# First loads in pieces on two queues, low halves of the first weights on VectorE, and another last stage, in a two-layer encoder kernel

## The chip, the cores and the metric

The kernel runs on one core of a Trainium2 chip. The metric is the time of one execution on the device in microseconds (us); a profile of one execution shows what each engine did. PE is TensorE, DVE VectorE, ACT ScalarE, POOL GpSimd, and SP the engine whose queue issues most transfers (DMAs).

## What is computed

Two layers over 1024 tokens of width 1024, in float32: windowed attention in layer 0, neighbourhood attention in layer 1, each with four heads over 256 memory tokens beside it, and a gated feed-forward part. The parts that the change touches:

```python
mem_n = rmsnorm(mem, norm_mem)
for i in range(DEPTH):                      # 2
    h = rmsnorm(x, norm_mix[i])
    mkv = mem_n @ w_mem_kv[i]               # keys and values of the memory
    proj = h @ (w_in_a if i % 2 == 0 else w_in_b)[i // 2]
    ...                                     # attention
    x = x + concat(y_tok, y_mem) @ w_out[i]
    h = rmsnorm(x, norm_ffn[i])
    gu = h @ w_gate_up[i]
    x = x + (silu(gu[..., :D_FF]) * gu[..., D_FF:]) @ w_down[i]
return rmsnorm(x, norm_final)
```

## The kernel before

**Layout.** Activations lie transposed: tile `x[k][f]` holds features 128k to 128k+127 of token half f (512 tokens). A product is made from operands split into a high half (float32r) and the rest: `hi` copies on ACT, `lo` subtracts (on DVE, or on POOL where `eng=nc.gpsimd` is given, then in four pieces), and each 128x128 block costs three matmuls (`three`). The tools' tile scheduler fixes each engine's instruction order when the program is built, and each engine works through its order without overtaking. SP issues the loads in its own order, and one that waits for a free buffer holds those behind it.

**Opening.** The pool `mp` holds the memory tokens `memt`. Eight units of memory keys and values follow (`i` from 0 to 7 in the loop): load a weight tile (`wm`, 512 KB, `load_w`), 24 matmuls of 256 columns against `mhl` (`dense`), scaling by `mscale` (`mt`), and for the value units a transpose (`mvT`, `mv`). Between them x is loaded and squared. The class `Norm` makes a root mean square: `add` squares a tile on ACT (`sq`) and merges it on DVE into two accumulators; `scale` merges these, sums over the partitions with matmuls against `inv_d` (`st`), adds epsilon (`nv`), takes the power on POOL (`nr`), builds a diagonal (`diag`) and broadcasts it by matmuls (`bc`). `split` then gives `h` and its halves `hT`. `first_dense` runs three units of the input projection on token half 0 (weights `wf`) while token half 1 is normalized; the same three units on half 1 follow, then the attention (scores `S`, probabilities `p`, transposes `pT`).

**End.** The down projection is done with seven products (`i` from 0 to 6, a Strassen scheme) of six groups of rows (`g` from 0 to 5). `left_side` loads and splits the weights (`wd_raw`, `wd`), `right_side` the operands (`b_raw`, `hB`), both two groups ahead. Weight tiles `wd` stand in a ring of three, raw tiles (`raw_tile`) in a ring of five here and of three in the opening. In the last group `product` runs over the four row blocks `m`, and `read` adds each block to x and hands it to `Norm`. `finish` scales a token half by `norm_final` and writes it in four pairs of tiles (512 KB each), all issued by SP, from a ring of two tiles `o`.

Of the kernel before, what the change touches and what calls it, by code (L numbers as in the profile page):

```python
# [41 lines left out]
def trunk_kernel(ctx: ExitStack, tc: tile.TileContext, a: dict, out: bass.AP):  # L42
# [110 lines left out]
    def first_dense(layer, norm):  # L153

        pre = []
        src = a["w_in_a"] if layer == 0 else a["w_in_b"]
        todo = (norm.add(x[k][1]) for k in range(len(norm.xs), NK))
        parts = norm.split(layer, hT[1])
        for n, u in enumerate(FIRST[layer]):
            w = load_w(src[u], eng=nc.gpsimd, name="wf")  # L160
            wide[:] = True, 2 + n
            ps = mm_tile()
            for i, _ in enumerate(steps(ps, w, hT[0])):
                if next(todo, 0) is not None and len(norm.xs) == NK and (n or i > 3):
                    next(parts, None)
            pre.append((w, ps))
        run(parts)
        return pre
# [15 lines left out]
    class Norm:  # L184


        def __init__(self, n=HS):
            self.n, self.acc, self.xs = n, [], {}

        def add(self, xk, k=None):  # L190

            n = self.n
            self.xs[len(self.xs) if k is None else k] = xk
            sq = temp("sq", n)
            nc.scalar.activation(sq, xk, AF.Square)
            self.acc.append(sq)
            if len(self.xs) > 2:
                self.merge()

        def merge(self):  # L200
# [4 lines left out]
        def scale(self):  # L205

            n, nb = self.n, self.n // P
            self.merge()
            st = ps_t.tile([P, HS], F32, tag="T", name="st")
            for b in range(nb):  # L210
                nc.tensor.matmul(
                    st[:, b : b + 1], self.acc[0][:, b * P : (b + 1) * P], inv_d, start=True, stop=True
                )
            v = sp.tile([P, 4], F32, tag="nv", name="nv", bufs=2)
# [40 lines left out]
    with tc.tile_pool(name="mp", bufs=1, reuse_waits="tile") as mp:  # L255
        phase[:] = mp, 5, 3
        memt = mp.tile([P, NK, NM], F32, name="memt")
        nc.sync.dma_start(gains, a["gains"])
        nc.sync.dma_start(memt[:, : NK // 2], a["mem"][:, : NK // 2])
        ws = [load_w(a["w_mem"][0, 0], name="wm", parts=2)]  # L260
        nc.sync.dma_start(memt[:, NK // 2 :], a["mem"][:, NK // 2 :])
        nc.sync.dma_start(ident, a["ident"])

# [3 lines left out]
        for k in range(NK):  # L267
# [4 lines left out]
            )  # L272
            mh.append(t)
        ws.append(load_w(a["w_mem"][0, 1], name="wm"))
        mem_norm = Norm(NM)
        for k in range(NK):
# [7 lines left out]
        for i in range(8):  # L284
# [6 lines left out]
            if i + 2 < 8:  # L291
                ws.append(load_w(a["w_mem"][(i + 2) // 4, (i + 2) % 4], name="wm", eng=nc.gpsimd))
            if i == 0:
                nc.sync.dma_start(sink, a["sink"].to_broadcast([P, NH]))
                nc.vector.tensor_scalar(nsink, sink, -1.0, None, op0=ALU.mult)
            if i in (0, 3):
                f = i // 3
                for k in range(NK):
                    x[k][f] = mp.tile([P, HS], F32, tag=f"x{k}{f}", name=f"x0_{k}{f}")
                    nc.sync.dma_start(x[k][f], a["x"][k][:, f * HS : (f + 1) * HS])  # L300
            ps = dense(ws[i], mh, NM)
# [5 lines left out]
            else:  # L307
# [5 lines left out]
                for b in range(2):  # L313
                    hi(vm[:, b, m : m + 2, 0], src[:, b])
                    lo(vm[:, b, m : m + 2, 1], src[:, b], vm[:, b, m : m + 2, 0])
            if i in (1, 2, 3, 4):
                for k in (2 * i - 2, 2 * i - 1):
                    norms[0].add(x[k][0])
            if i == 4:
                parts = norms[0].split(0, hT[0])  # L320
            if i >= 4:
                run_some(parts, 2)
                for k in (2 * i - 8, 2 * i - 7):
                    norms[1].add(x[k][1])
# [6 lines left out]
    for layer in range(2):  # L331
# [427 lines left out]
        with tc.tile_pool(name=f"fp{layer}", bufs=1, reuse_waits="tile") as fp:  # L759
# [381 lines left out]
            def finish(norm, at):  # L1141

                bc = norm.scale()
                for k in range(NK):
                    if k % 2 == 0:
                        o = fp.tile([P, 2, HS], F32, tag="S", bufs=2, name="o")
                    nc.vector.scalar_tensor_tensor(
                        o[:, k % 2], norm.xs[k], gains[:, 5, k : k + 1], bc, op0=ALU.mult, op1=ALU.mult
                    )
                    if k % 2 == 1:  # L1150
                        nc.sync.dma_start(out[k - 1 : k + 1].rearrange("k p t -> p k t")[:, :, at : at + HS], o)
                    yield
# [12 lines left out]
            for at_, (i, g) in enumerate(dorder):  # L1165
# [22 lines left out]
                if i == 6:  # L1188
# [98 lines left out]
```

## Time and profile before

| | |
|---|---|
| three runs, us | 2201.31, 2204.14 (median), 2206.15 |
| profiled execution: time, span, us | 2205.49, 2202.5 |
| PE busy in the span | 2129.8 us (97%) |
| DVE, ACT, POOL busy | 1440.2, 1056.5, 673.9 us (65, 48, 31%) |

The span is what the profile shows from the first to the last instruction of the one execution; its time is 3.0 us longer. Busy times are averages over stages: what an edit is worth is read from the stage in which it lies. In the sections below an idle time and what ended it stand in square brackets at the end of a row.

### The profile page before, as it was taken

Reading aid. Unit: us, or ns where it says so; the run is one execution under the profiler, and the core shown is the slowest. Engines: PE = TensorE matmul, PEld = TensorE weight load, DVE = VectorE, ACT = ScalarE, POOL = GpSimd, SP = SyncE. Lnnn points to the kernel's source line nnn. Section 1 sums busy time; section 2 is a strip of 40 time slices with the busy share of each in tenths; the row PEclk is TensorE's granted clock in tenths of the full one; section 3 lists DMA queues with packets and bytes.
Section 4 is the critical chain, followed back from the end, with each engine's and each line's share of the span. In section 5 each row is a group of like instructions: output and inputs, shape, how many; then the busy total and the mean of one; then the engine's idle time right before and its main releaser. Section 6 shows DMA issues by size and latency. Waiting matters only on the chain.

```text
span 2202.5 us, 28160 instructions
## 1 busy us (share of the span) xinstructions
PE 2129.8 (97%) x9930; PEld 1749.9 (79%) x9930; DVE 1440.2 (65%) x2241; ACT 1056.5 (48%) x2016; POOL 673.9 (31%) x647
## 2 busy tenths in 40 slices
PE   6899999999999999999999999999999999999996
PEld 6688888788888887787788888887888888877875
DVE  5677787776555456767866666667865555567575
ACT  5477785443333333445466566653433333334442
POOL 4334330323332321363233233202233233213540
PEclk8999999999999999999999999999999999999998
DMA  6312117423223236766332222274232232366562
GB/s 221 119 39 82 49 58 268 133 82 122 97 93 110 100 115 225 248 208 215 111 91 72 76 65 86 64 263 139 82 101 110 96 115 96 120 225 229 178 234 81
DMA packets 117020, 287.21 MB, mean 130 GB/s; under 512 B 12304, under 2 KB 18704, under 8 KB 116880
## 3 DMA queue, kind: packets, MB, share of 16 engines
q1 hardware_dynamic: 110544, 273.89, 36.9%
q10 hardware_dynamic: 6336, 11.54, 1.4%
q8 instruction: 78, 1.28, 0.2%
q14 instruction: 62, 0.51, 0.1%
HBM read 210.40 MB, written 68.94 MB: 127 GB/s over the span
## 4 chain that ended last, share of the span: by engine, by line
PE 73%; issue 10%; DVE 6%; ACT 4%; DMA 4%; POOL 3%; SPq 0%; POOLq 0%; DVEq 0%; ACTq 0%
PE X L844 21%; PE Y L844 16%; PE mm L139 13%; PE X L1136 6%; PE po L139 4%; PE S L524 3%; PE Y L1136 3%; PE O L587 3%; PE pT L567 2%; DMA b_raw<-b_d 1%; DVE hB L109 1%; ACT p L539 1%; POOL x L1096 1%; DVE wd L109 1%; DMA wd_kept<-in_w_dn 1%
## 5 line engine op out<-in xcount | busy, mean ns | idle before, releaser
L844 PE MATMUL X<-hT,wgu 128*128 128x512 f32 x1056 | 259.0, 395 | 0.0
L844 PE MATMUL Y<-hB,wgu 128*128 128x512 f32 x1056 | 256.3, 392 | 0.0
L1136 PE MATMUL X<-hB,wd 128*128 128x512 f32 x1056 | 248.3, 395 | 7.0 <-DVE c L852 3.4
L844 PE MATMUL X<-hB,wgu 128*128 128x512 f32 x1056 | 247.8, 390 | 0.0
L1136 PEld LDWEIGHTS X<-hB,wd 128*128 128x128 f32 x1056 | 200.2, 190 | 52.9 <-DVE c L852 4.3
L844 PEld LDWEIGHTS X<-hT,wgu 128*128 128x128 f32 x1056 | 198.2, 188 | 47.2
L552 POOL TENSOR_SCALAR p<-p,stat 128x384 f32<-128x384 f32 (+1 forms) x256 | 140.9, 570 | 309.8 <-DVE stat L549 206.6
L844 PEld LDWEIGHTS Y<-hB,wgu 128*128 128x128 f32 x1056 | 198.5, 188 | 43.9 <-issue 1.5
L844 PEld LDWEIGHTS X<-hB,wgu 128*128 128x128 f32 x1056 | 198.3, 188 | 41.8
L106 ACT CAST wgu<-wS 128x1024 fp32r<-128x1024 f32 x88 | 92.5, 1051 | 259.7 <-POOL wS L803 157.1
L109 DVE TENSOR_TENSOR wgu<-wgu_raw,wgu 128x1024 fp32r<-128x1024 f32 (+1 forms) x88 | 85.7, 974 | 190.3 <-ACT wgu L106 190.3
L139 PE MATMUL mm<-hT,wqk 128*128 128x512 f32 x672 | 199.8, 405 | 0.1
L1136 PE MATMUL Y<-hB,wd 128*128 128x512 f32 x792 | 185.2, 395 | 8.9 <-DVE hB L109 4.5
L803 POOL TENSOR_TENSOR wS<-wgu_raw 128x512 f32<-128x512 f32 x44 | 73.6, 1672 | 379.0 <-DVE wgu L109 379.0
L139 PE MATMUL po<-yT,wo 128*128 128x512 f32 x768 | 184.7, 394 | 0.0
L1136 PEld LDWEIGHTS Y<-hB,wd 128*128 128x128 f32 x792 | 150.6, 191 | 42.6 <-DVE hB L109 5.3
L109 DVE TENSOR_TENSOR hB<-b_raw,hB 128x512 fp32r<-128x512 f32 x154 | 131.9, 892 | 53.1 <-ACT hB L106 52.9
L139 PEld LDWEIGHTS po<-yT,wo 128*128 128x128 f32 x768 | 142.4, 188 | 29.5 <-issue 1.0
L109 DVE TENSOR_TENSOR wgu<-wS,wgu 128x1024 fp32r<-128x1024 f32 x88 | 109.7, 1247 | 62.6 <-ACT wgu L106 62.6
L539 ACT ACTIVATE p<-p,stat 128x256 f32<-128x256 f32 (+1 forms) x192 | 112.4, 586 | 51.1 <-DVE stat L535 48.5
L810 POOL TENSOR_TENSOR wS<-wgu_raw 128x512 f32<-128x512 f32 x44 | 58.3, 1326 | 251.2 <-DMA wgu_raw<-in_w_gu 197.5
L106 ACT CAST hB<-b_raw 128x512 fp32r<-128x512 f32 x154 | 88.8, 619 | 95.4 <-DMA b_raw<-b_d 95.3
(158 smaller groups left out, 4026.8 us busy)
## 6 DMA issues: line engine op xcount, KB each, us to landing
wgu_raw<-in_w_gu SPq DMA_DIRECT2D x92, 512.0 KB
b_raw<-b_d SPq DMA_DIRECT2D x70, 512.0 KB
wd_raw<-in_w_dn SPq DMA_DIRECT2D x50, 512.0 KB
b_d<-c SPq DMA_DIRECT2D x88, 256.0 KB
b_d<-t SPq DMA_DIRECT2D x66, 256.0 KB
wo_raw<-in_w_out SPq DMA_DIRECT2D x32, 512.0 KB
wd_kept<-in_w_dn SPq DMA_DIRECT2D x10, 1024.0 KB
x<-in_x SPq DMA_DIRECT2D x32, 256.0 KB
```

The costliest lines, as they stand in the source:

```text
L106: nc.scalar.copy(dst, src)
L109: (eng or nc.vector).tensor_tensor(dst, src, h.bitcast(F32), op=ALU.subtract)
L139: nc.tensor.matmul(ps[:, :n], l, r, start=start and i == 0 and j == 0, stop=stop and i == len(order) - 1 and j == 2,)
L524: nc.tensor.matmul(s_[:, :n], Q[self.h][:, qb * P : (qb + 1) * P], k, start=j == 0, stop=j == 1)
L539: nc.scalar.activation(p[:, :n], p[:, :n], AF.Exp, bias=m1, scale=-1.0, accum_out=s1)
L552: nc.gpsimd.tensor_scalar(p[:, :n], p[:, :n], ri[:, i : i + 1], 1.0, op0=ALU.mult, op1=ALU.mult)
L567: nc.tensor.transpose(tr[:, j * P : (j + 1) * P], p[:, j * P : (j + 1) * P], ident)
L587: nc.tensor.matmul(o[:, c0 : c0 + w * P], self.value(j), t[:, s0 : s0 + w].rearrange("p j q -> p (j q)"), start=j == js[0] and t is self.p ...
L803: sub = lambda o, p_, q_: nc.gpsimd.tensor_tensor(o, p_, q_, op=ALU.subtract)
L810: nc.gpsimd.tensor_tensor(s[:, HS:], u1, u2, op=ALU.add)
L844: nc.tensor.matmul(ps, l, r, start=n in (0, 1, 3, 6) and k == 0 and i == 0, stop=k == 3 and i == 2, skip_group_check=True,)
L1136: nc.tensor.matmul(bank, l, r, start=i in (0, 1, 3, 6) and p == 0 and n == 0, stop=p == HF - 1 and n == 2, skip_group_check=True,)
```

## The change

In the opening the memory tokens come in three pieces (two, two and four of the eight feature blocks) instead of two halves, the first weight tile in two halves issued by ACT, and the table of ACT's functions is loaded by a small square of a constant tile ahead of any data. The low halves of the memory weights and of layer 0's first three projection weights are made on DVE instead of POOL. The loads of x are spread over the units 0 to 6, token half 0 is squared at the units 1 and 2 (four tiles each), and its `split` starts after unit 2. The pool has 8 temporaries instead of 5 and 5 raw tiles instead of 3.

At the end, groups 4 and 5 of the last product are done block by block: all nine matmuls of one row block, then the next. In layer 1's last token half the eighth square isn't merged: both accumulators and that square go to PE, twelve matmuls against `inv_d` where there were four. The tiles `o` come from the ring of raw tiles; in the last half two of the eight products are made on POOL (from tiles already scaled by the gain on ACT, and from a copy `bs` of the broadcast), the last two tiles go out singly on SP and ACT, and the first pair goes out on ACT.

```diff
-            w = load_w(src[u], eng=nc.gpsimd, name="wf")
+            w = load_w(src[u], eng=None if layer == 0 else nc.gpsimd, name="wf")
...
     class Norm:
-        def __init__(self, n=HS):
-            self.n, self.acc, self.xs = n, [], {}
+        def __init__(self, n=HS, summed=NK):
+            self.n, self.acc, self.xs, self.st = n, [], {}, None
+            self.summed = summed
 
         def add(self, xk, k=None):
...
             nc.scalar.activation(sq, xk, AF.Square)
+            if len(self.xs) > self.summed:
+                while self.acc:
+                    self.mean(self.acc.pop(0))
+                self.mean(sq)
+                return
             self.acc.append(sq)
             if len(self.xs) > 2:
                 self.merge()
+
+        def mean(self, sq):
+
+            start = self.st is None
+            if start:
+                self.st = ps_t.tile([P, HS], F32, tag="T", name="st")
+            for b in range(self.n // P):
+                nc.tensor.matmul(
+                    self.st[:, b : b + 1], sq[:, b * P : (b + 1) * P], inv_d,
+                    start=start and b == 0, stop=True, skip_group_check=True,
+                )
...
         def scale(self):
...
+            if len(self.acc) > 1:
+                self.merge()
+            for sq in self.acc:
+                self.mean(sq)
+            st = self.st
...
-        phase[:] = mp, 5, 3
+        phase[:] = mp, 8, 5
         memt = mp.tile([P, NK, NM], F32, name="memt")
+        warm = mp.tile([P, P], F32, name="warm")
+        nc.scalar.activation(warm, ones, AF.Square)
+        wm0 = raw_tile("wm0")
+        nc.sync.dma_start(memt[:, :2], a["mem"][:, :2])
+        nc.scalar.dma_start(wm0[:, :HS], a["w_mem"][0, 0][:, :HS])
         nc.sync.dma_start(gains, a["gains"])
-        nc.sync.dma_start(memt[:, : NK // 2], a["mem"][:, : NK // 2])
-        ws = [load_w(a["w_mem"][0, 0], name="wm", parts=2)]
-        nc.sync.dma_start(memt[:, NK // 2 :], a["mem"][:, NK // 2 :])
-        nc.sync.dma_start(ident, a["ident"])
+        nc.sync.dma_start(memt[:, 2:4], a["mem"][:, 2:4])
+        nc.scalar.dma_start(wm0[:, HS:], a["w_mem"][0, 0][:, HS:])
+        nc.sync.dma_start(memt[:, 4:], a["mem"][:, 4:])
+        w0 = wp.tile([P, 2, D], F32R, tag="whl", name="wm", bufs=3)
...
-                ws.append(load_w(a["w_mem"][(i + 2) // 4, (i + 2) % 4], name="wm", eng=nc.gpsimd))
+                ws.append(load_w(a["w_mem"][(i + 2) // 4, (i + 2) % 4], name="wm"))
...
-            if i in (0, 3):
...
+            if i < 3:
+                for k in ((0, 1, 2), (3, 4, 5), (6, 7))[i]:
+                    load_x(0, k)
+            elif i < 7:
+                for k in (2 * i - 6, 2 * i - 5):
+                    load_x(1, k)
...
-            if i in (1, 2, 3, 4):
-                for k in (2 * i - 2, 2 * i - 1):
+            if i in (1, 2):
+                for k in range(4 * i - 4, 4 * i):
                     norms[0].add(x[k][0])
-            if i == 4:
+            if i == 2:
                 parts = norms[0].split(0, hT[0])
-            if i >= 4:
+            if i > 2:
                 run_some(parts, 2)
-                for k in (2 * i - 8, 2 * i - 7):
+            if i in (5, 6):
+                for k in range(4 * i - 20, 4 * i - 16):
                     norms[1].add(x[k][1])
...
             def finish(norm, at):
 
                 bc = norm.scale()
+                last = at > 0
+                if last:
+                    bs = temp("bs")
+                    nc.scalar.copy(bs, bc)
                 for k in range(NK):
                     if k % 2 == 0:
-                        o = fp.tile([P, 2, HS], F32, tag="S", bufs=2, name="o")
...
+                        o = raw_tile("o").rearrange("p (k t) -> p k t", k=2)
+                    if last and k < 2:
+                        nc.gpsimd.tensor_tensor(o[:, k], norm.xs[k], bs, op=ALU.mult)
+                    else:
...
+                    yield
+                    if last and k > 5:
+                        queue = nc.scalar if k % 2 else nc.sync
+                        queue.dma_start(out[k][:, at : at + HS], o[:, k % 2])
+                    elif last and k == 1:
+                        first = o
...
+                if last:
+                    nc.scalar.dma_start(out[:2].rearrange("k p t -> p k t")[:, :, at:], first)
...
-            norms = [Norm(), Norm()]
+            norms = [Norm(), Norm() if is_a else Norm(HS, 7)]
...
                     for m in range(4):
-                        product(i, m, p, bank[m])
+                        for q in range(p - 2 if i == 6 else p, HF):
+                            product(i, m, q, bank[m])
                         read(i, m, bank[m])
+                elif g == len(groups) - 2 and i == 6:
+                    pass
...
                         norms[1].add(x[g][1], g)
+                        if not is_a and g < 2:
+                            nc.scalar.mul(x[g][1], x[g][1], gains[:, 5, g : g + 1])
```

Three places in the instruction orders. The first is DVE in the memory units, from the third transposed pair to the diagonal of token half 0; `wm` is the subtraction of a weight tile, `mt` the scaled unit, `sq` a merge. Before:

```order
L109 TENSOR_TENSOR mv_188<-mvT,mv_188 128x2x64
L202 TENSOR_TENSOR sq<-sq 128x512
L109 TENSOR_TENSOR mv_188<-mvT,mv_188 128x2x64
L303 TENSOR_TENSOR mt<-mm,mscale 128x256
L202 TENSOR_TENSOR sq<-sq 128x512 x2
L109 TENSOR_TENSOR mv_188<-mvT,mv_188 128x2x64 x2
L303 TENSOR_TENSOR mt<-mm,mscale 128x256
L202 TENSOR_TENSOR sq<-sq 128x512
L109 TENSOR_TENSOR mkl_398<-mt,mkh_397 128x256
L202 TENSOR_TENSOR sq<-sq 128x512 x2
L216 TENSOR_SCALAR nv<-st 128x4
L219 TENSOR_TENSOR diag<-ident,nr 128x512
```

And in the changed kernel:

```order
L109 TENSOR_TENSOR wm<-wm_raw,wm 128x1024
L109 TENSOR_TENSOR mv_192<-mvT,mv_192 128x2x64
L219 TENSOR_TENSOR sq<-sq 128x512
L109 TENSOR_TENSOR mv_192<-mvT,mv_192 128x2x64
L219 TENSOR_TENSOR sq<-sq 128x512 x3
L109 TENSOR_TENSOR wm<-wm_raw,wm 128x1024
L337 TENSOR_TENSOR mt<-mm,mscale 128x256
L219 TENSOR_TENSOR sq<-sq 128x512
L109 TENSOR_TENSOR wm<-wm_raw,wm 128x1024
L109 TENSOR_TENSOR mv_192<-mvT,mv_192 128x2x64
L232 TENSOR_SCALAR nv<-st 128x4
L235 TENSOR_TENSOR diag<-ident,nr 128x512
```

The subtractions of three weight tiles, which stood on POOL, now stand between the merges, and one scaled unit fewer (with the second pair `mv` of its transposes) stands ahead of the diagonal.

The second is PE around the two broadcasts `bc` of x, up to the first scores of the attention. Before:

```order
L139 MATMUL mm<-mhl,wm 128x256
L226 MATMUL bc<-diag,ones 128x512
L139 MATMUL mm<-mhl,wm 128x256 x47
L139 MATMUL mm<-hT,wf 128x512 x12
L310 MATMUL mvT<-ident,mt 128x128 x2
L139 MATMUL mm<-hT,wf 128x512 x6
L310 MATMUL mvT<-ident,mt 128x128 x2
L139 MATMUL mm<-hT,wf 128x512 x22
L211 MATMUL st<-inv_d,sq 128x1 x4
L139 MATMUL mm<-hT,wf 128x512 x6
L226 MATMUL bc<-diag,ones 128x512
L139 MATMUL mm<-hT,wf 128x512 x98
```

And now, from the row right behind the first broadcast:

```order
L139 MATMUL mm<-mhl,wm 128x256 x49
L139 MATMUL mm<-hT,wf 128x512 x2
L139 MATMUL mm<-mhl,wm 128x256 x22
L139 MATMUL mm<-hT,wf 128x512 x10
L344 MATMUL mvT<-ident,mt 128x128 x2
L139 MATMUL mm<-hT,wf 128x512 x12
L344 MATMUL mvT<-ident,mt 128x128 x2
L139 MATMUL mm<-hT,wf 128x512 x2
L212 MATMUL st<-inv_d,sq 128x1 x4
L139 MATMUL mm<-hT,wf 128x512 x13
L242 MATMUL bc<-diag,ones 128x512
L139 MATMUL mm<-hT,wf 128x512 x105
```

Behind the first broadcast (`mm<-mhl` is a matmul of a memory unit, `mm<-hT` one of the projection) now stand 71 matmuls of the memory units instead of 47, in two lots, and behind the second 105 matmuls of the projection instead of 98.

The third is SP's end, the last weights and operands of the last product and the outputs. Before:

```order
L1068 DMA b_raw<-b_d_99 128x1024
L1014 DMA wd_raw<-in_w_dn 128x2x512 x2
L1068 DMA b_raw<-b_d_99 128x1024
L1014 DMA wd_raw<-in_w_dn 128x2x512
L1068 DMA b_raw<-b_d_99 128x1024 x2
L1014 DMA wd_raw<-in_w_dn 128x512
L1068 DMA b_raw<-b_d_99 128x1024
L1068 DMA b_raw<-b_d_99 128x512
L1151 DMA out<-o 128x2x512 x8
```

And now:

```order
L1103 DMA b_raw<-b_d_99 128x1024
L1049 DMA wd_raw<-in_w_dn 128x2x512
L1103 DMA b_raw<-b_d_99 128x1024 x4
L1103 DMA b_raw<-b_d_99 128x512
L1049 DMA wd_raw<-in_w_dn 128x2x512
L1199 DMA out<-o 128x2x512
L1049 DMA wd_raw<-in_w_dn 128x2x512
L1199 DMA out<-o 128x2x512
L1049 DMA wd_raw<-in_w_dn 128x512
L1199 DMA out<-o 128x2x512 x4
L1195 DMA out<-o 128x512
```

The last three weight loads stand behind all operand loads, two of them behind an output each.

## Rows read from the trace of the kernel before

**Rows 1.** Busy time by stretch: opening, second half of it, last output stage.
```profile
core 0: us, PE busy (x) PEld busy (x) DVE busy (x) ACT busy (x) POOL busy (x), PEclk, DMA share, GB/s
...
0.00:26.00 26.00, 14.82 (x82) 13.14 (x82) 13.79 (x31) 14.04 (x30) 4.64 (x10) 0.93 0.87 306
...
46.85:74.65 27.80, 24.08 (x108) 19.00 (x108) 21.68 (x33) 12.42 (x23) 16.32 (x19) 0.82 0.49 157
...
2191.60:2202.50 10.90, 0.00 (x0) 0.00 (x0) 5.43 (x8) 0.00 (x0) 0.00 (x0) 0.50 0.51 193
```

**Rows 2.** Chain that ended last, first load; then timeline, opening to the memory scale.
```profile
1.17 4.51 DMA memt<-in_mem
...
5.75 1.28 ACT L269 ACT_TABLE_LOAD   x1 [5.75 <-DMA memt<-in_mem]
...
8.49 2.90 ACT L269 ACTIVATE mhl<-memt,gains 128x256 fp32r<-128x256 f32 x7
...
11.29 1.03 ACT L106 CAST wm<-wm_raw 128x1024 fp32r<-128x1024 f32 x1
...
12.23 1.03 ACT L195 ACTIVATE sq<-memt 128x256 f32<-128x256 f32 x3
...
12.36 1.23 DVE L109 TENSOR_TENSOR wm<-wm_raw,wm 128x1024 fp32r<-128x1024 f32 x1 [0.20 <-ACT wm L106]
...
13.50 1.09 DVE L202 TENSOR_TENSOR sq<-sq 128x256 f32<-128x256 f32 x3
...
14.89 3.35 POOL L109 TENSOR_TENSOR wm<-wm_raw,wm 128x256 fp32r<-128x256 f32 x4 [14.46 <-ACT wm L106]
...
15.16 3.36 DVE L202 TENSOR_TENSOR sq<-sq 128x256 f32<-128x256 f32 x4 [0.48 <-ACT sq L195]
...
21.94 0.37 ACT L279 COPY mscale<-bc 128x256 f32<-128x256 f32 x1 [6.20 <-PE bc L226]
```

**Rows 3.** Timeline, memory units up to the first normalized tile of x.
```profile
23.45 1.15 ACT L195 ACTIVATE sq<-x 128x512 f32<-128x512 f32 x2
...
33.78 6.56 PE L139 MATMUL mm<-mhl,wm 128*128 128x256 f32 x43
...
42.43 1.02 POOL L217 TENSOR_TENSOR nr<-nv,neg_half 128x4 f32<-128x4 f32 x1 [7.09 <-PE mm L139]
...
46.85 1.41 DVE L243 SCALAR_TENSOR_TENSOR h<-x,gains,bc 128x512 f32<-128x512 f32 x2 [2.17 <-PE bc L226]
```

**Rows 4.** Timeline, second sum of squares and what stands behind it.
```profile
73.52 1.13 PE L226 MATMUL bc<-diag,ones 128*128 128x512 f32 x2 [0.57 <-DVE diag L219]
...
74.08 22.83 PE L139 MATMUL mm<-hT,wf 128*128 128x512 f32 x98
...
74.69 2.07 DVE L243 SCALAR_TENSOR_TENSOR h<-x,gains,bc 128x512 f32<-128x512 f32 x3 [1.22 <-PE bc L226]
...
76.67 1.89 DVE L109 TENSOR_TENSOR hT<-h,hT 128x512 fp32r<-128x512 f32 x3
```

**Rows 5.** Timeline, opening of the attention of layer 0.
```profile
103.90 2.76 POOL L109 TENSOR_TENSOR wqq<-wqq_raw,wqq 128x256 fp32r<-128x256 f32 x4
...
107.18 1.55 PE L567 MATMUL pT<-ident,p 128*128 128x128 f32 x6 [3.30 <-POOL p L552]
```

**Rows 6.** Timeline, last product to the last output; then the chain, one output transfer.
```profile
2154.84 1.05 PE L211 MATMUL st<-inv_d,sq 128*128 128x1 f32 x8
...
2159.45 21.44 PE L1136 MATMUL X<-hB,wd 128*128 128x512 f32 x92
...
2167.33 0.62 ACT L106 CAST wd<-wd_raw 128x512 fp32r<-128x512 f32 x1 [4.38 <-PE X L1136]
...
2185.51 1.87 PE L211 MATMUL st<-inv_d,sq 128*128 128x1 f32 x8 [4.62 <-DVE sq L202]
...
2195.87 2.75 DVE L1147 SCALAR_TENSOR_TENSOR o<-x,gains,bc 128x512 f32<-128x512 f32 x4 [1.58 <-DMA out<-o]
...
2192.99 2.78 DMA out<-o
```

More of the change, by code (lines that the diff above doesn't have):

```diff
@@ L207, in scale @@
             n, nb = self.n, self.n // P
[L208 to L213, printed above, removed]
+            if len(self.acc) > 1:
[3 more added lines that the diff above has]
+            st = self.st
             v = sp.tile([P, 4], F32, tag="nv", name="nv", bufs=2)
@@ L255, in trunk_kernel @@
     with tc.tile_pool(name="mp", bufs=1, reuse_waits="tile") as mp:
-        phase[:] = mp, 5, 3
+        phase[:] = mp, 8, 5
         memt = mp.tile([P, NK, NM], F32, name="memt")
-        nc.sync.dma_start(gains, a["gains"])
-        nc.sync.dma_start(memt[:, : NK // 2], a["mem"][:, : NK // 2])
-        ws = [load_w(a["w_mem"][0, 0], name="wm", parts=2)]
-        nc.sync.dma_start(memt[:, NK // 2 :], a["mem"][:, NK // 2 :])
-        nc.sync.dma_start(ident, a["ident"])
+        warm = mp.tile([P, P], F32, name="warm")
[3 more added lines that the diff above has]
+        nc.scalar.dma_start(wm0[:, :HS], a["w_mem"][0, 0][:, :HS])
+        nc.sync.dma_start(gains, a["gains"])
+        nc.sync.dma_start(memt[:, 2:4], a["mem"][:, 2:4])
+        nc.scalar.dma_start(wm0[:, HS:], a["w_mem"][0, 0][:, HS:])
+        nc.sync.dma_start(memt[:, 4:], a["mem"][:, 4:])
+        w0 = wp.tile([P, 2, D], F32R, tag="whl", name="wm", bufs=3)
+        hi(w0[:, 0, :HS], wm0[:, :HS])
+        lo(w0[:, 1, :HS], wm0[:, :HS], w0[:, 0, :HS])
+        ws = [w0]
         mh = []
@@ L273, in trunk_kernel, with load_x @@
             mh.append(t)
+            if k == 1:
+                hi(w0[:, 0, HS:], wm0[:, HS:])
+                lo(w0[:, 1, HS:], wm0[:, HS:], w0[:, 0, HS:])
         ws.append(load_w(a["w_mem"][0, 1], name="wm"))
+        nc.sync.dma_start(ident, a["ident"])
+        def load_x(f, k):
+            x[k][f] = mp.tile([P, HS], F32, tag=f"x{k}{f}", name=f"x0_{k}{f}")
+            nc.sync.dma_start(x[k][f], a["x"][k][:, f * HS : (f + 1) * HS])
         mem_norm = Norm(NM)
@@ L295, in trunk_kernel @@
                 nc.vector.tensor_scalar(nsink, sink, -1.0, None, op0=ALU.mult)
-            if i in (0, 3):
[L297 to L300, printed above, removed]
+            if i < 3:
[4 more added lines that the diff above has]
+                    load_x(1, k)
             ps = dense(ws[i], mh, NM)
@@ L1143, in finish @@
                 bc = norm.scale()
+                last = at > 0
+                if last:
+                    bs = temp("bs")
+                    nc.scalar.copy(bs, bc)
                 for k in range(NK):
                     if k % 2 == 0:
-                        o = fp.tile([P, 2, HS], F32, tag="S", bufs=2, name="o")
[L1147 to L1150, printed above, removed]
+                        o = raw_tile("o").rearrange("p (k t) -> p k t", k=2)
+                    if last and k < 2:
+                        nc.gpsimd.tensor_tensor(o[:, k], norm.xs[k], bs, op=ALU.mult)
+                    else:
+                        nc.vector.scalar_tensor_tensor(
+                            o[:, k % 2], norm.xs[k], gains[:, 5, k : k + 1], bc, op0=ALU.mult, op1=ALU.mult
+                        )
+                    yield
[4 more added lines that the diff above has]
+                        first = o
+                    elif k % 2 == 1:
                         nc.sync.dma_start(out[k - 1 : k + 1].rearrange("k p t -> p k t")[:, :, at : at + HS], o)
-                    yield
+                if last:
+                    nc.scalar.dma_start(out[:2].rearrange("k p t -> p k t")[:, :, at:], first)
             for u, n in gate_up():
```

## The prediction

> **What bounds the kernel now.** I read the page first: PE is busy 97% of the span, so an edit pays only where PE waits. The busy time by stretch shows where that is: in the first 26 us PE works 14.8 us, and in the last 10.9 us it does nothing [rows 1]. Both ends are touched by the change. Then the chain and the timeline of the opening, to see what each wait is for. The first load takes 4.51 us, and only when it has landed does ACT load its function table, 1.28 us more [rows 2]. From there the opening is a relay: ACT makes high halves, DVE or POOL low halves, PE uses both, and squares and merges stand between them in the same in-order queues. The first normalized tile `h` comes at 46.85, the second broadcast ends at 74.65, the last of the 98 products behind it at 96.91 [rows 3, 4]. From 46.85 on DVE is busy 21.68 of 27.80 us and POOL 16.32 [rows 1]. Last I read the end: products end at 2180.89, the sum of squares at 2187.38, the last `o` at 2198.62 [rows 6].
>
> **The opening, up to the memory scale.** The pieces are half the size of the first load and are issued some 0.45 us earlier. They land at 0.7 + 4.51 = 5.2 us at the latest, if size gives nothing, and at 0.7 + 2.78 = 3.5 us at the earliest, the time of a 512 KB output at the end [rows 2, 6]; I take 4.2 between them. The table load lies under it: 1.28 us off the path. ACT then has a half weight cast (0.5), three `mhl` (2.90/7 = 0.41 each), a half cast, five `mhl`: 4.2 + 1.0 + 3.3 = 8.5. The next cast takes 1.03, to 9.55, eight squares 0.34 each to 12.3, a third cast to 13.3 [rows 2]. DVE subtracts the second tile by 10.8 (1.23 each, against 3.35 on POOL), PE does 22 products behind that at 6.56/43 = 0.153, to 14.2, and the third subtraction ends at 14.55 [rows 2, 3]. From the last merge to the end of `mscale` it was 18.52 to 22.31, 3.8 us [rows 2]; from 14.3 that gives 18.1. Gain 4.2, and 3.2 if the pieces land as late as 5.2.
>
> DVE takes nine subtractions from POOL, 9 x 1.23 = 11.1 us. What pays for part of that is that POOL falls silent: merges of 256 columns took 1.09/3 = 0.36 each before POOL started and 3.36/4 = 0.84 while it worked [rows 2].
>
> **Memory units up to the first `h`.** From the broadcast (17.7) PE has 37 matmuls at 0.153, to 23.4, and two transposes, to 23.8. Then, by the new order, ACT copies a transposed piece, squares three tiles, copies another, squares the last: I take 0.3 for a small piece (a merge of 256 columns takes 0.36) and 0.58 for a square [rows 2, 3], together 2.9, to 26.7. A cast to 27.7; DVE, through with the merges at about 28.0, subtracts that weight tile (1.23), scales a unit (0.4, also next to that merge), merges (1.89/3 = 0.63, the rate of a 512-column DVE operation here), to 30.3. This is the new head-of-line wait: PE's next transposes need that scaled unit, which stands behind a weight subtraction in DVE's order, and PE idles from some 24.6 to 29.7. The sum on PE takes 1.05 [rows 6], DVE meanwhile subtracts another tile, to 31.5, and a small piece, 31.8. Then epsilon 0.2, POOL's power 1.02, the diagonal 0.7, the broadcast 1.13, gaps 0.2: `h` at 35.1 instead of 46.85 [rows 3, 4]. Gain so far 11.7. Data hold: the seventh weight tile is cast at 27.7, and all bytes ahead of it, 7.4 MB (1.05 of memory, seven tiles of 0.52, ten and more of x at 0.26), land by 24.2 at the 306 GB/s of the first 26 us [rows 1].
>
> **Up to the first scores.** DVE is now the engine that sets the pace. By its order it has, up to the second epsilon, 8 `h` at 2.07/3 = 0.69, 8 `hT` at 0.63 and 7 merges at 0.63 [rows 4], three weight subtractions at 1.23, and nine small operations of 0.3 to 0.4: 5.5 + 5.0 + 4.4 + 3.7 + 3.1 = 21.7 us. With 1 us of waits, for which ACT's queue gives reason, that ends at 57.8. A subtraction (1.23) hides POOL's power; with it a small piece, the diagonal, the broadcast and the gaps 3.6 us, to 61.4, where before it was 74.65. Gain 13.2. But 105 matmuls instead of 98 stand behind it, at 22.83/98 = 0.233: 61.4 + 24.5 = 85.9 instead of 96.91 [rows 4]. Token half 1 is ready for them: its eight `h` and `hT` take 8 x 1.32 = 10.6 us on DVE, the first 33 of the matmuls are on half 0, and a step of three takes 0.7. **Term 1: 11.0 us.** Bounds: if DVE's operations ran as slowly as under POOL, or a wait of 3 us stood in each of the two long legs, 5; if every leg ran without its waits, 15.
>
> **Opening of the attention.** PE stood 3.30 us for the first probabilities, which POOL made only after the low half of a later weight tile, 2.76 us [rows 5]. In the new order four probabilities go ahead of it. The tile then delays the second four, and four matmuls fewer cover the wait. **Term 2: 1.5 us**, from 0 to 3.
>
> **The end.** Product 6 keeps its 132 matmuls. What changes is the distance of the blocks: nine matmuls, 21.44/92 x 9 = 2.1 us, instead of three, 0.7, so each add, square and merge (0.69 + 0.58 + 0.63) is done before the next block. After 2180.89 only one add and one square are left, 1.5 us with gaps; PE meanwhile sums the two accumulators, 2 x 1.05 at the rate of the sum right behind matmuls, and then the last square, 1.05: 3.2 us to the end of the sum instead of 6.49 [rows 6]. Gain 3.3. It would be 3.9 if the accumulators cost nothing, 0.9 if PE ran all at the 1.87 seen after an idle stretch. The chain epsilon, power, diagonal, broadcast I leave at its 4.1 us.
>
> From the broadcast's end to the last `o` it was 7.1 us, eight operations and a wait of 1.58 for an output to free the ring of two [rows 6]. Six operations at 0.69 now end at 4.1, and the two on POOL beside them do not end later unless POOL takes over 1.7 each. That would be 3.0 us, but the transfers have to drain: 2.1 MB left at 193 GB/s with the transfer engines 0.51 busy [rows 1], which makes 378 GB/s at full share and 5.6 us. The first pair is issued 1.4 after the broadcast; with 2.78 - 1.4 of fixed time the last byte lands 8.4 us after it, where the old last one landed 7.1 + 2.78 = 9.9 after it. So the transfers take back half: gain 1.5 to 3.4, I take 2.0. The Trainium skill, DMA: Bandwidth & Descriptors, section Issuing engines are not separate DMA queues, speaks against the two queues here: transfers issued by SP and ACT run on the same 16 engines and interleave, so only issue time is saved. By it the output gains the 1.5 of the drain alone, and the sum would be 17.3 instead of 17.8; no trace of before shows ACT and SP issuing at once at the end.
>
> **Term 3: 5.3 us**, from 2.4 to 8. Edits at no cost: the two multiplications by the gain on ACT, 1.2 us, lie under product 6, where ACT works in single microseconds; if uncovered they would cost just that. In layer 0 the same block order is used, but PE has the next products to go on with; I take nothing.
>
> **Sum.** 11.0 + 1.5 + 5.3 = 17.8 us. The profiled execution took 2205.49 us, 1.35 above the median of 2204.14; 2187.7 against its own time is 2186.3 against the median. A measurement of this kernel can tell about 0.2%, 4.4 us, from no change.
>
> **Rivals.** (a) DVE takes the opening back: the 11.1 us of moved subtractions come fully onto the path in the two long legs, so that only the first leg's 4.2 is kept and the 6.8 behind it is lost. For it speaks that DVE's sum of 21.7 already fills its leg; against it that DVE worked 21.68 in that leg before, too, with slower operations. Gain 4.2 + 1.5 + 5.3 = 11: 2193. (b) The opening is bound by loads: x and the weights arrive 4 us later than I need them, since 0.87 of the transfer engines is already in use in the first 26 us [rows 1]. Gain 13.8: 2190.3. (c) The output split does nothing, since the drain sets the end: 2187.8, or 2189 if POOL's two operations run long. (d) Slower: the last 256 KB of weights stand in SP's queue behind two outputs, and its buffer is one that the first output frees. That output starts at some 2161.6 and lands at 2164.4, the load at 2167, cast and subtraction end at 2168.7; the cast waited for its weight buffer until 2167.33 anyway, and the first block that needs it begins 36 matmuls, 8.4 us, before the end, at 2172.5 [rows 6]. So there are 3.8 us to spare, and every microsecond beyond is paid. It decides only if the load is late by 3.8 + 17.8 + 4.4 = 26 us; nothing in the trace makes it so.
>
> **How the numbers follow.** My forecast (gain of 13 to 23 us, with (b) and (c) near its lower edge) 0.65; more than that, all legs without waits and a faster broadcast at the end, 0.08; (a), and mixtures with a smaller end, gain 5 to 13, 0.20; no difference that can be told 0.05; (d) or the like 0.02. The time is that of the likeliest. The range takes the upper bounds of the terms (15 + 3 + 8 = 26) at one side and the lower 5 + 0 + 4 at the other: 2178 to 2195.
>
> **What would show it.** Right: ACT's table load before 3 us; the first `h` near 35; the first scores near 86; POOL nearly silent before; a sum of squares that ends 3.2 us after the last product; last `o` 4 us after the broadcast. Wrong: DVE without gaps from 20 to 60 and the first scores after 91; a PE wait before the first block of the last product; outputs that land 9 us and more after the broadcast.

## The result, and the profile after

The changed kernel took 2189.74 us (median of 6 runs, 2184.95 to 2194.44) against 2203.42 (6 runs): ratio 0.9938, 95% interval 0.9922 to 0.9955, a gain of 13.7 us. Two later measurements, on two chips, gave 0.9933 [0.9921, 0.9946] and 0.9929 [0.9916, 0.9942], by the ratio 14.8 and 15.6 us; gains below are by the ratio too. The forecast was 17.8: the direction and the range held, the size was 2 to 4 us too large. The profiled execution took 2190.96 us, its span is 2189.1.

First the opening: windows of the changed kernel for the first 26 us, from the first `h` to the end of the second broadcast, and for the last output stage, as in [rows 1].

```profile
core 0: us, PE busy (x) PEld busy (x) DVE busy (x) ACT busy (x) POOL busy (x), PEclk, DMA share, GB/s
0.00:26.00 26.00, 16.04 (x106) 14.67 (x106) 18.41 (x41) 19.71 (x39) 0.90 (x5) 1.00 0.93 341
35.15:59.65 24.50, 21.17 (x125) 16.96 (x124) 22.57 (x39) 14.21 (x26) 1.85 (x1) 1.00 0.20 66
2178.87:2189.10 10.23, 0.00 (x0) 0.00 (x0) 4.04 (x6) 0.58 (x1) 2.50 (x2) 0.50 0.56 205
```

POOL has fallen silent (1.85 us where it had 16.32), DVE is busy 22.57 of 24.50. The timeline of the same stretch, and of the opening of the attention:

```profile
1.17 1.28 ACT L275 ACT_TABLE_LOAD   x1 [1.17 <-PEq L1330]
...
4.88 0.62 ACT L106 CAST wm<-wm 128x512 fp32r<-128x512 f32 x1 [2.11 <-DMA wm<-in_w_mem]
...
25.39 0.51 PE L139 MATMUL mm<-mhl,wm 128*128 128x256 f32 x2 [3.18 <-ACT wm L106]
...
27.57 0.64 PE L344 MATMUL mvT<-ident,mt 128*128 128x128 f32 x2
...
35.15 1.41 DVE L259 SCALAR_TENSOR_TENSOR h<-x,gains,bc 128x512 f32<-128x512 f32 x2 [2.88 <-PE bc L242]
...
55.35 3.22 PE L139 MATMUL mm<-hT,wf 128*128 128x512 f32 x13
...
58.52 1.13 PE L242 MATMUL bc<-diag,ones 128*128 128x512 f32 x2
...
83.31 0.28 PE L559 MATMUL S<-mKH,QS 128*128 128x256 f32 x1
```

The table load lies under the first transfer, the first cast starts at 4.88, the first `h` at 35.15 (46.85 in [rows 3]), the second broadcast ends at 59.65 (74.65 in [rows 4]), the first scores come at 83.31 where they came at 96.75. The probabilities reach PE 7.98 us after the first scores instead of 10.43.

The end, as in [rows 6]:

```profile
2150.86 21.68 PE L1171 MATMUL X<-hB,wd 128*128 128x512 f32 x93
...
2172.37 2.74 PE L212 MATMUL st<-inv_d,sq 128*128 128x1 f32 x24
...
2175.15 0.16 DVE L232 TENSOR_SCALAR nv<-st 128x4 f32<-128x4 f32 x1 [1.89 <-PE st L212]
...
2177.18 1.68 PE L242 MATMUL bc<-diag,ones 128*128 128x512 f32 x2 [2.07 <-DVE diag L235]
2178.95 0.58 ACT L1182 COPY bs<-bc 128x512 f32<-128x512 f32 x1 [5.03 <-PE bc L242]
2179.57 4.04 DVE L1189 SCALAR_TENSOR_TENSOR o<-x,gains,bc 128x512 f32<-128x512 f32 x6 [2.45 <-ACT bs L1182]
2179.67 2.50 POOL L1187 TENSOR_TENSOR o<-x,bs 128x512 f32<-128x512 f32 x2 [3.27 <-ACT bs L1182]
...
2183.64 0.36 ACTq L1195 DMA_DIRECT2D out<-o  x1
```

The products end at 2172.53, the sum of squares 2.6 us later instead of 6.5. But a new wait stands in the output stage: DVE's first `o` starts only when ACT has copied the broadcast, 0.7 us after the broadcast itself. From the last product to the end of the span it is 16.6 us, before 21.6.

So the two ends gained 15.9 us at the first transposed probabilities (107.18 to 91.29) and 5.0 at the end, but the spans differ by 13.35 only. The rest is given back between. To see where, each of ScalarE's instructions was set against the same instruction in the first profile of the kernel before; the lead below is the median over those of a 20 us stretch (times of the kernel before), the first and the last two columns are from PE's rows and the span.

```
profile                        107   200   440  1060  1120  last X  span
before, second profile        -0.3   0.2  -0.8   0.3   0.3  -2.6   -2.6
end alone                      2.2   2.2   1.0   2.2   0.6   2.1    6.7
changed, first                15.9  14.3  10.9   8.8   7.2   8.4   13.4
changed, second               12.9  11.4  11.5   9.9   8.3   9.1   14.2
changed, third                13.3  12.5  12.4  13.8  12.3  11.6   16.2
opening alone                 13.9  13.1  10.2  11.4  11.2  11.1   11.2
changed, old blocks, layer 0  15.4  13.8  11.1  11.3  10.8  12.6   17.5
the same, second broadcast    13.3  12.5   9.3   9.1   8.7   9.3   14.8
```

### The profile page after: what moved, and what is told of

It reads as the page before. It is cut to its first block, busy times and chain, and to the rows that moved or that the text cites. A ratio compares the mean times of both kernels' runs of the same rounds, so it can differ in the third digit from the quotient of the medians.

```text
span 2189.1 us, 28147 instructions
## 1 busy us (share of the span) xinstructions
PE 2124.1 (97%) x9946; PEld 1745.9 (80%) x9946; DVE 1441.6 (66%) x2246; ACT 1059.5 (48%) x2020; POOL 649.0 (30%) x613
## 4 chain that ended last, share of the span: by engine, by line
PE 78%; issue 8%; DVE 6%; ACT 4%; DMA 2%; POOL 1%; SPq 0%; DVEq 0%; ACTq 0%; POOLq 0%
PE X L879 21%; PE Y L879 16%; PE mm L139 13%; PE X L1171 9%; PE Y L1171 5%; PE po L139 4%; PE S L559 3%; PE O L622 3%; PE pT L602 2%; DVE sq L219 1%; DVE hB L109 1%; ACT p L574 1%; DMA wd_kept<-in_w_dn 1%; DMA wd_raw<-in_w_dn 1%; DVE pl L109 1%
```

## The experiments

The theory after the first comparison was that the lead is cut systematically, at layer 0's out projection and at the turns to gate/up and down; the rival, that these cuts are jitter of one execution.

**The two halves alone, and both kernels again.** The first has the changed opening with the old `finish` and product loop, the second the old opening with the changed end; both have the changed class `Norm`.

> The changed opening with the old end. Landmarks if the parts are independent: first scores near 83 us as in the changed kernel (96.75 before), last product to end of span near 21.6 us as before. Theory A (the gain of the opening, 13.4 us at the first scores and 15.9 at the first probabilities, is systematically cut on the way, at layer 0's out projection and at the turns to gate/up and down): total gain 7 to 10 us, near 2195, and the products end no more than 9 us earlier than before. Rival B (those cuts are jitter of the one profiled execution): total gain 13 to 16 us, near 2189.

Measured: 0.9953 [0.9941, 0.9966], a gain of 10.4 us, between what the two theories gave; first scores at 85.26, last product to end 21.5.

> The old opening with the changed end. First scores near 97 us as before; last product to end of span near 16.6 us instead of 21.6. Both theories: total gain 4.5 to 6 us, near 2198. If only 0 to 3 us come, the end takes something back that the two profiles do not show (block order in layer 0, the multiplications by the gain on ScalarE).

Measured: 0.9990 [0.9978, 1.0002], 2.2 us, under both theories' 4.5 to 6 and not clear of no change; first scores at 94.59, last product to end 17.0. Its profile keeps 4.6 us of the end, but the lead falls by 1.6 between 1060 and 1120 (table), where the prediction had taken nothing.

> The changed kernel once more, for a second profile. Theory A: the broadcast behind layer 0's out projection again starts only after PE stood about 2 us for VectorE's diagonal, ScalarE again waits some 2 to 3 us for a gate/up weight tile there, and the lead over the kernel before again shrinks from about 15 us at 110 us to 11 at 410 and 8 to 9 at 850. Rival B: another execution loses elsewhere or not at all there, and the lead at 410 us is 14 or more, or the loss stands at other places. Time near 2190 again, gain 11 to 16.

> The kernel before once more, for a second profile: how far its landmarks move from one execution to the next. Theory A: the broadcast at 384.6, gate/up at 421.8, the first down product at 850 and the last product at 2180.9 move by less than 1.5 us against the first profile. Rival B: they move by 3 us or more against each other.

Measured: the second profile of the changed kernel loses nothing between 200 and 440, where the first lost 3.4, but its first scores come at 86.27. The kernel before moves by 2.6 us at the last product, which lies between the two theories. So the loss at the out projection comes and goes: there ACT waited for a weight tile 2.79 us in the first profile and 0.86 in the second, and only in the first stood PE for the diagonal:

```profile
367.06 1.05 ACT L106 CAST wgu<-wgu_raw 128x1024 fp32r<-128x1024 f32 x1 [2.79 <-DMA wgu_raw<-in_w_gu]
...
372.01 2.05 PE L242 MATMUL bc<-diag,ones 128*128 128x512 f32 x2 [2.18 <-DVE diag L235]
```

```profile
367.72 1.05 ACT L106 CAST wgu<-wgu_raw 128x1024 fp32r<-128x1024 f32 x1 [0.86 <-DMA wgu_raw<-in_w_gu]
...
373.04 1.10 PE L242 MATMUL bc<-diag,ones 128*128 128x512 f32 x2 [0.22 <-DVE diag L235]
```

(first and second profile of the changed kernel). The theory fell for that place. It held for another: between 1060 and 1120 all nine profiles with the new block order in layer 0 lose 1.5 to 1.8.

**The turn of the layers.**

```diff
-                        for q in range(p - 2 if i == 6 else p, HF):
+                        for q in range(p - 2 if i == 6 and not is_a else p, HF):
-                elif g == len(groups) - 2 and i == 6:
+                elif g == len(groups) - 2 and i == 6 and not is_a:
```

> The changed kernel, with the old order of the last two row groups of product 6 in layer 0 alone (layer 1 keeps the new order). In three profiles with the new order in layer 0 the lead over the kernel before falls by 1.2 to 1.6 us between 1060 and 1110 us, in the one without it by nothing. Theory A (the block order costs that at the turn of the layers, where the prediction took nothing): the lead falls by less than 0.4 us there, and the time is 1 to 2 us under the changed kernel's 2189.5. Rival: the loss comes from where PE's clock happens to stand there, and it stays at 1.2 or more.

Measured: 2187.31 us, 0.9918 [0.9900, 0.9936], which doesn't stand clear of the changed kernel's ratios. The lead falls by nothing up to 1110, the stretch of the expectation, in this profile and in the two others with the old order and the new opening, and by 0.5, 0.4 and 0.1 up to 1120; in the three profiles of the changed kernel it falls by 1.5 up to either. The cause stands in PE's rows behind layer 0's last product, first of the changed kernel, then of this one:

```profile
1070.33 3.94 PE L139 MATMUL mm<-hT,wf 128*128 128x512 f32 x16
1075.14 1.05 PE L212 MATMUL st<-inv_d,sq 128*128 128x1 f32 x8 [0.87 <-DVE sq L219]
1076.06 1.64 PE L139 MATMUL mm<-hT,wf 128*128 128x512 f32 x6
1078.78 1.13 PE L242 MATMUL bc<-diag,ones 128*128 128x512 f32 x2 [1.08 <-DVE diag L235]
```

```profile
1067.48 5.07 PE L139 MATMUL mm<-hT,wf 128*128 128x512 f32 x21
1072.39 0.95 PE L212 MATMUL st<-inv_d,sq 128*128 128x1 f32 x8
1073.20 1.62 PE L139 MATMUL mm<-hT,wf 128*128 128x512 f32 x6
1075.91 1.13 PE L242 MATMUL bc<-diag,ones 128*128 128x512 f32 x2 [1.09 <-DVE diag L235]
```

From the first of these matmuls to the broadcast both take 8.4 us. In that time PE does 22 matmuls in the new order and 27 in the old; the program now puts the sum five matmuls earlier, but the merges are not done earlier, so PE waits 0.87 us and five matmuls, 5 x 0.24 = 1.2 us, are left behind the broadcast, most of the loss.

**The opening, one edit at a time undone.** In the eight profiles with the opening unchanged the first scores come at 83.3 to 87.0, mean 85.2; in the three with the old one at 94.6 to 97.0, mean 96.1.

```diff
-            w = load_w(src[u], eng=None if layer == 0 else nc.gpsimd, name="wf")
+            w = load_w(src[u], eng=nc.gpsimd, name="wf")
-                ws.append(load_w(a["w_mem"][(i + 2) // 4, (i + 2) % 4], name="wm"))
+                ws.append(load_w(a["w_mem"][(i + 2) // 4, (i + 2) % 4], name="wm", eng=nc.gpsimd))
```

> The changed kernel, with the low halves of the weight tiles (six of the memory units, three of the first projections) subtracted by GpSimd in four pieces, as before. Theory A (VectorE does them in a third of the time, and its other operations run at full rate when GpSimd is silent): first normalized tile at 38 to 41 instead of 35.1, first scores at 89 to 94 instead of 83 to 86, total 2195 to 2199. Rival (the work only moves, VectorE is the engine that sets the pace and pays for it what GpSimd saves): first scores within 2 us of 83 to 86.

Measured: first scores at 91.52, as the theory has it, but first `h` at 36.82 and 2192.93 us (0.9941 [0.9920, 0.9962]), both under its ranges. The theory held only for the second half of the opening: there PE waits for a scaled unit that DVE makes late, behind three merges that took 1.2 us each while POOL worked, and 0.69 each in the changed kernel.

```profile
50.11 7.96 POOL L109 TENSOR_TENSOR wf<-wf_raw,wf 128x256 fp32r<-128x256 f32 x8 [2.08 <-ACT wf L106]
```

```profile
55.15 3.47 DVE L219 TENSOR_TENSOR sq<-sq 128x512 f32<-128x512 f32 x3
```

```profile
59.01 0.53 PE L344 MATMUL mvT<-ident,mt 128*128 128x128 f32 x2 [3.00 <-DVE mt L337]
```

Not all of these 6.3 us (against the mean of 85.2) are kept: PE's wait for the first probabilities is nil here, so at the first transposed probabilities this profile is 4.6 us behind the mean of the eight, and at 200 us 3.0.

The next kernel has the five lines of the old first loads in place of the new ones (from `warm` to `ws`), without the second half cast in the loop.

> The changed kernel with the old first loads: gains first, memory in two halves, the first weight tile whole, all on SyncE, no early table load. Theory A (a relay, so the first leg's gain goes through whole): memory scale copied at 21.5 to 22.5 instead of 17.7, first normalized tile 39 to 40, first scores 4 to 5 us later than in the changed kernel, 88 to 90, total 2193 to 2195. Rival (the next legs wait for loads or VectorE, which hides it): first scores at most 2 us later.

Measured: memory scale copied by 20.68, first `h` at 39.61, first scores at 89.31: 4.1 over the mean, as the relay has it, though the profiles with the opening unchanged differ by 3.6 among themselves. The first leg lost 2.4 to 3.0 only. Time 2190.83 (0.9937 [0.9914, 0.9960]), under the 2193 to 2195.

```diff
-            if i < 3:
-                for k in ((0, 1, 2), (3, 4, 5), (6, 7))[i]:
-                    load_x(0, k)
-            elif i < 7:
-                for k in (2 * i - 6, 2 * i - 5):
-                    load_x(1, k)
+            if i in (0, 3):
+                for k in range(NK):
+                    load_x(i // 3, k)
...
-            if i in (1, 2):
+            if i in (1, 2, 3, 4):
...
-            if i == 2:
+            if i == 4:
```

> The changed kernel with the loads of x, its squares and the norm placed as before (half 0 loaded in the first unit and squared over units 1 to 4, half 1 from unit 3 on). Theory A (the first norm is early because its squares stand two units earlier): memory scale still 17.7, first normalized tile 41 to 44 instead of 35.1, first scores 91 to 96, total 2196 to 2201. Rival (VectorE's subtractions set the pace, the order does not matter): first tile before 38, first scores before 88.

Measured: first `h` at 39.20, but first scores at 86.96, 1.8 over the mean and inside the range of the others; 2191.00 us (0.9932 [0.9907, 0.9958]), under the 2196 to 2201. Theory A was too high in all three, and the rival had the first tile before 38 and so held for the first scores only. The first norm comes 3 to 4 us later, but PE then does more projection matmuls before the second broadcast: 94 stand behind it instead of 105, 2.6 us less.

The times of these three can't be told from the changed kernel's; the landmarks of single profiles carry the verdicts.

**The end, one part at a time undone.**

```diff
-            norms = [Norm(), Norm() if is_a else Norm(HS, 7)]
+            norms = [Norm(), Norm()]
```

> The changed kernel, but VectorE merges the last square and the two accumulators again, as before; block order and output stay new. Theory A (the new distance of the blocks and PE's summing each give part): the sum of squares ends 4 to 5 us after the last product, where it was 6.49 before and 2.6 with both, and last product to end of span takes 18.2 to 19 us instead of 16.5 to 17.3. Rival (the distance of the blocks alone does it): the sum ends by 3.2 us after the last product.

Measured, in one run: the epsilon behind the sum starts 4.0 us after the last product, which ends at 2173.46 (6.5 before, 2.6 with both edits), and it is 19.0 to the end of the span.

```profile
2176.35 1.05 PE L212 MATMUL st<-inv_d,sq 128*128 128x1 f32 x8 [2.89 <-DVE sq L219]
...
2177.44 0.16 DVE L232 TENSOR_SCALAR nv<-st 128x4 f32<-128x4 f32 x1 [1.14 <-PE st L212]
```

So the distance of the blocks gives 2.5 of the 3.9 us, PE's summing 1.4.

The next has the old `finish` and no multiplications by the gain.

> The changed kernel with the old output stage: eight products on VectorE, pairs on SyncE, a ring of two, no multiplications by the gain on ScalarE. Theory A (the transfers set the end of the new stage, its start is late by the 0.7 us of ScalarE's copy): end of the broadcast to end of span 10.8 to 11 us as before, where the changed kernel shows 10.3 in both profiles, so 0.5 to 0.8 us of difference. The prediction's step said 2.0; rival (the split does nothing): within 0.3.

Measured, in one run: 10.88 us from the end of the broadcast, at 2180.39, to the end of the span at 2191.27. The four profiles with the old output stage show 10.85 to 10.98, the nine with the changed one 9.97 to 10.88, median 10.26, and 10.26 to 10.28 in the three of the changed kernel. The whole output edit is worth 0.6 to 0.7 us. Then the wait for ACT's copy was taken away, on top of the old blocks in layer 0:

```diff
+                    bt = ps_t.tile([P, HS], F32, tag="T", name="bt")
+                    nc.tensor.matmul(bt, ones, norm.dg, start=True, stop=True)
                     bs = temp("bs")
-                    nc.scalar.copy(bs, bc)
+                    nc.scalar.copy(bs, bt)
```

> The changed kernel with the old block order in layer 0, and at the end a second broadcast into another bank of PSUM, from which ScalarE copies, so that VectorE need not wait for that copy. Theory A: VectorE's first output product starts within 0.1 us of the broadcast's end instead of 0.7, the last byte lands some 0.6 us earlier, end of the broadcast to end of span 9.6 to 9.9 instead of 10.3; total about 2 us under the changed kernel on the same chip. Rival (the transfers or GpSimd's two products set the end): 10.2 to 10.5 as before, total 1.4 us under it.

Measured: DVE starts 0.04 us after the broadcast, and the stage takes 9.35 us in this one profile instead of 10.3, less than theory A's 9.6 to 9.9:

```profile
2176.28 2.05 PE L242 MATMUL bc<-diag,ones 128*128 128x512 f32 x2 [2.06 <-DVE diag L235]
2178.12 1.83 PE L1183 MATMUL bt<-diag,ones 128*128 128x512 f32 x2
2178.37 4.04 DVE L1192 SCALAR_TENSOR_TENSOR o<-x,gains,bc 128x512 f32<-128x512 f32 x6 [2.15 <-PE bc L242]
```

> The changed kernel a third time, on the same chip as the version above. Time near 2189.5, 1 to 3 us over the version above. At the turn of the layers the lead over the kernel before falls by 1.2 to 1.6 us as in its two other profiles; at layer 0's out projection the loss is anything from 0 to 3 us if it is jitter, and 2 to 3 us if it belongs to the change.

Measured: 2189.36 us (2181.21 to 2191.57) with both edits and 2187.97 (2185.20 to 2189.34) for the changed kernel beside it, both 0.9929 of before. The 2 us that the trace shows for the two edits are less than these runs can tell, since the way between varies by more, and the 1 to 3 us that were expected didn't come; no version is shown to beat the changed kernel.

## Why the prediction was right or wrong

**Term 1, 11.0 us: right in size, in part by luck.** The first profile shows 13.4, but the means over the three profiles with the old opening and the eight with the new one are 96.1 and 85.2, a difference of 10.9. The landmarks came close: scale copied by 17.66 (18.1), first `h` 35.15 (35.1), second broadcast ends 59.65, in the mean of the eight 61.5 (61.4). But the hit at the first `h` is two errors that cancel. PE's wait, put at 24.6 to 29.7, comes earlier, 3.2 us up to 25.39, and is for a weight tile's cast, which stands behind squares of x in ACT's order, not for the scaled unit behind DVE's subtraction; the epsilon starts at 30.09 and not at 31.8. Then the step let the broadcast follow the diagonal at once, but in PE's order 19 products of a memory unit stand ahead of it. They ran behind that wait at a granted clock of 0.50 (1.2 GHz, 30 to 34 us), 0.23 us each where the step had 0.153, and the broadcast starts 2.0 us after the diagonal's end:

```profile
28.22 1.83 PE L212 MATMUL st<-inv_d,sq 128*128 128x1 f32 x8
...
29.91 4.34 PE L139 MATMUL mm<-mhl,wm 128*128 128x256 f32 x19
...
31.38 0.69 DVE L235 TENSOR_TENSOR diag<-ident,nr 128x512 f32<-128x512 f32 x1 [1.13 <-POOL nr L233]
...
34.08 1.03 PE L242 MATMUL bc<-diag,ones 128*128 128x512 f32 x2
```

Rival (a) is excluded: the legs behind the first kept their gain (10.9 in all, not 4.2), and putting the subtractions back on POOL costs 6 us at the first scores and 3 at 200 us. Rival (b) too, though loads were near: 341 GB/s in the first 26 us, a cast that waited 2.25 us for its weight tile at 15.96, and yet no late first scores.

**Term 2, 1.5 us: right; the landmarks show 2.45.** From the first scores to the first transposed probabilities it is 10.43 or 10.44 in three profiles with the old opening and 7.98 or 7.99 in eight with the new one. PE's wait there fell from 3.30 [rows 5] to 1.81:

```profile
91.29 1.60 PE L602 MATMUL pT<-ident,p 128*128 128x128 f32 x6 [1.81 <-POOL p L587]
```

That is 1.49 us. The other 0.96 is the four matmuls of the next projection that the step named: 13 of them stand in this stretch instead of 17. They were moved behind the transposes, not saved.

**Term 3, 5.3 us: 4.6 to 5.1 in seven profiles with the whole new end and 4.3 in the eighth, from parts that were off both ways.** The sum of squares ends 2.6 after the last product, not 3.2: PE sums the accumulators beside the last add and square, so the gain is 3.9 instead of 3.3. The output stage gains 0.7 instead of 2.0, below the bound of 1.5. The drain itself was sized well:

```profile
2180.00:2182.00 2.00, 0.00 (x0) 0.00 (x0) 2.00 (x4) 0.00 (x0) 2.00 (x2) 0.50 0.06 22
2182.00:2187.00 5.00, 0.00 (x0) 0.00 (x0) 1.61 (x3) 0.00 (x0) 0.17 (x1) 0.50 1.03 379
```

379 GB/s at full share, where 378 was worked out. What failed is the start: the step took DVE's first `o` to follow the broadcast, but ACT's copy of the same PSUM tile comes first, 0.7 us. The last output's landing in the trace says the same: 9.1 us after the broadcast (2187.94), where the step had 8.4 and the prediction named 9 and more as a sign of being wrong; with the second broadcast it lands after 8.4. The old one landed after 9.9, so without the copy ahead the gain is the 1.5 of the drain, and the 2.0 that was taken was too much even then. The Trainium skill, DMA: Bandwidth & Descriptors, section Issuing engines are not separate DMA queues, has it that SP's and ACT's transfers share the same engines; the trace agrees, 379 GB/s from both together. Rival (d) didn't occur: PE has no wait over 0.3 us from 2150 to the last product.

**"In layer 0 the same block order is used, but PE has the next products to go on with; I take nothing": wrong, shown.** It costs 1.0 to 1.5 us, some 1.2 (1.5 against nothing by 1110 and 0.1 to 0.5 by 1120). PE does have other products, but fewer of them stand ahead of the sum in its order.

**The step that was never written: that the way between passes a lead on unchanged.** In the attention of layer 0 0.8 to 1.7 us go between 107 and 200 in every profile that has the new opening in full, and nothing where it is the old one. About 0.7 of it is two waits in PE's rows of the changed kernel, where the kernel before has none and 0.07 us at the same operations.

```profile
152.60 0.52 PE L602 MATMUL pT<-ident,p 128*128 128x128 f32 x3 [0.38 <-DVE pl L109]
...
163.65 0.45 PE L559 MATMUL S<-KH,QS 128*128 128x384 f32 x1 [0.37 <-DVE stat L570]
```

The rest is the four matmuls of Term 2, and PE's clock decides whether they are seen. In the 5 us from the first transposes on the granted clock is 0.66 or 0.67 in the five profiles that lose 1.5 to 1.7 and in all three with the old opening, and 1.00 in the three that lose 0.8. Here are the first profile of the changed kernel and the one of the opening alone:

```profile
91.29:96.29 5.00, 4.96 (x21) 3.97 (x21) 1.81 (x6) 1.72 (x6) 4.55 (x9) 0.66 0.00 0
```

```profile
93.25:98.25 5.00, 4.74 (x25) 3.21 (x25) 2.54 (x8) 2.62 (x8) 5.00 (x10) 1.00 0.00 0
```

For the two waits the cause is argued, not shown: the order of the instructions there changes with the opening, which would give DVE's results later. With the subtractions back on POOL the second wait is gone and the first still there (0.41).

The account: 10.9 + 2.45 + 5.0 = 18.3, less 1.2 at the turn of the layers and about 1.3 in the attention, 15.8. Measured were 13.7, 14.8 and 15.6, with intervals of some 3 us each way. Between 200 and 1060 the lead falls by 2.4 us in the mean of the eight profiles with the new opening, though from a loss of 5.5 to a gain of 1.3 in three profiles of one and the same kernel, and by nothing in the two others with the old opening. So that way seems to cut a lead too; with it the account comes to 13.4, and the measured gains lie between. What does it there stays open: no experiment took it apart.

Three of the prediction's sums don't add up, and nothing hangs on them: rival (c), without the 2.0 of the output, is 2188.3 and not 2187.8; the slow edge of the range takes 4 for Term 3, whose own lower bound was 2.4, which gives 2196.7 and not 2195; and its upper bound of 8 is over its parts, 3.9 + 3.4.

## What to carry to other kernels

A gain at one end is only worth what the rest of the program passes on; before summing terms, look in the new order for sums and broadcasts that have fewer products ahead of them. When two landmarks move together, count the work between them: part of the gain may be work that was moved behind the second. A change in the order of blocks that shortens the tail where nothing follows can cost in the layer where something does (1.5 us of lead here), so try it in the tail alone. When an engine is to help with an output, look whether its copy shares a PSUM tile with the engine that it helps.

## What the hardware showed that was not expected

The same program ran one stretch of the opening at both of PE's clock levels. Windows of the changed kernel, first and second profile, from 54 to 61 us, after a stretch in which PE had stood 1.41 us:

```profile
54.00:61.00 7.00, 7.00 (x34) 5.31 (x33) 5.08 (x9) 1.06 (x3) 1.85 (x1) 1.00 0.38 128
```

```profile
54.00:61.00 7.00, 7.00 (x23) 5.90 (x23) 3.84 (x7) 0.53 (x2) 1.85 (x1) 0.52 0.24 85
```

The granted share was 1.00 (2.4 GHz) in one and 0.52, nearly all at 1.2 GHz, in the other; the 13 matmuls ahead of the second broadcast took 3.22 and 5.10 us, and the first scores came 3.0 us apart, though both had their first `h` within 0.1. One profile of either kernel would have given that term as 13.4 or as 10.5.
